# A recurrence in three operations per step with one source in PSUM, its scratch bank opened behind the parameters, and urgent rotary work for queries

## The chip, the cores and the metric

The kernel runs on one core of a Trainium2 chip. The metric is the device time of one execution in microseconds. Engines: PE is TensorE (matmul), DVE is VectorE, ACT is ScalarE, POOL is GpSimd, SP is SyncE, whose queue issues most DMAs.

## What is computed

One backbone layer over 1024 latent tokens and 256 context tokens of width 1024, in float32. A projection of the modulated, normed input gives queries, keys, values, the input of a state space model (S5) and gates:

```python
z = modulate(x, p['norm1_w'], sh1, sc1) @ w_in
q = rms_norm(z[..., Q_OFF:K_OFF].reshape(b, l, N_HEADS, 2, HEAD_DIM), p['q_norm_w'])
k = rms_norm(z[..., K_OFF:V_OFF].reshape(b, l, N_HEADS, 2, HEAD_DIM), p['k_norm_w'])
v = z[..., V_OFF:U_OFF].reshape(b, l, N_HEADS, V_DIM)
u = z[..., U_OFF:G_OFF]
g = z[..., G_OFF:]
q = rope_2d(q, rope)
k = rope_2d(k, rope)
...
y_attn = diff_head_out(blocked_latent_diff_attention(q, k_all, v_all, lam),
                       p['subln_w'], lam_init, p['w_branch_attn'])
y_s5, y_s5_c = s5_branch(u, uc, p, update_ctx)
x = x + ga1 * merge_branches(g, y_s5, y_attn, p['b_gate'], p['w_out'])
x = x + ga2 * conv_ffn(modulate(x, p['norm2_w'], sh2, sc2), p['w_up'], p['conv_w'], p['conv_b'], p['w_down'])
```

The S5 branch is a complex diagonal recurrence s' = a s + b u per channel group, once forwards and once backwards over the tokens, that starts from the final state of the context.

## The kernel before, in words

Every projection is made with operands split into a high and a low part: three matmuls (`whi,hTh`, `wlo,hTh`, `whi,hTl`; L418 to L420) for each of 8 slices of the width, so 24 of 512 columns for one tile `z` of 128 tokens by 512 outputs (`project`). `load_slab` loads a weight slab of 512 outputs as four pieces `wraw`; ScalarE makes `whi` of it, GpSimd `wlo` (L597).

`phase_a` takes the slabs in this order: U; K (two slabs, 10 tiles each: 8 of latent, 2 of context tokens); V (two, 10 tiles each); Q (two, 8 tiles each); then the gates G (four slabs, L555 to L557). `phase_b` is the attention and `phase_c` the feed-forward part; neither is touched.

While K runs, the generator `params` (`s5_params`) makes the matrices of the S5 branch. VectorE computes `ba` and `ca` (L753 to L758, last L841); TensorE transposes `ba` (L846) and multiplies `ca` and `sc` into a bank named `ada` (L864). The S5 branch works on chunks of 8 tokens: `s5_states_in` brings the input of every chunk into `X` (while V runs), and `s5_scan` then carries the state over 158 chunks, each step in four operations of VectorE on [128, 64] (L936 to L939), the factors `A8a` and `A8b` in SBUF. `phase_a` asks for ten steps per V tile once the states are there, for six steps per Q tile, and for the rest after Q.

For each Q tile, `qk_post` does the norm and the rotary part: ScalarE squares `z`; VectorE sums (L642), makes the mean square (L643), and after ScalarE's root the reciprocal and a correction (L647 to L650); VectorE multiplies `z` by the cosine and the sine table (L654, L658); GpSimd adds the two (L659) and scales by `qr` (L665); TensorE transposes the result `t` into `ta` or `tb` (L669); ScalarE and VectorE write it as a high and a low part `st` (L672, L673), which go to DRAM as `Qd`.

Between Q tiles stand pieces of `ada_part`, the modulation of the later stages: each loads 512 KB (`araw`, two buffers) and multiplies it into the bank `ada` (L297). Gate tiles are evicted by ScalarE into `stage` (L559).

PSUM has 8 banks: two of the pool `psT` (`ta`, `tb`), and in `psA` five buffers `z` and one `ada` in this part.

The order of the instructions on each engine is not written by hand here. A scheduler sets it when the program is built, from the program order, priorities and its own notion of when operands come; the hardware then runs each engine's instructions strictly in that order. A tile is the unit of its dependencies: two users of one tile keep their program order. A pool that is closed hands its memory on, and what is opened in its place waits for the last use of what was there.

Of the kernel before, what the change touches and what calls it, by code (L numbers as in the profile page):

```python
# [13 lines left out]
OP = mybir.AluOpType  # L14
AX = mybir.AxisListType
PSUM = bass.MemoryType.PSUM
DRAM = bass.MemoryType.DRAM

P = 128
# [8 lines left out]
HD = 64  # L28
G = 32
# [5 lines left out]
EPS = 1e-6  # L35
# [103 lines left out]
class Kern:  # L139
# [81 lines left out]
    def consts(self):  # L221
        nc, cp = self.nc, self.cp
        self.small = self.t(cp, [P, NSM], "small")
        self.ident = self.t(cp, [P, P], "ident")
        self.ones = self.t(cp, [P, P], "ones")
        nc.vector.memset(self.ones, 1.0)
        self.onesr = self.t(cp, [P, P], "onesr", 1, F32R)
        nc.vector.tensor_copy(self.onesr, self.ones)
        self.modT = self.t(cp, [P, 48, 2], "modT")
        self.neglam = self.t(cp, [P, 1], "neglam")  # L230
        self.hbg = self.t(cp, [P, 16], "hbg")
        self.hglub = self.t(cp, [P, 4], "hglub")
        self.subw = self.t(cp, [P, 1], "subw")
        self.scan_at = 0
# [78 lines left out]
    def phase_a(self):  # L313
        nc, cp, I = self.nc, self.cp, self.I
        self.psT, self.psT_st = self.pool("psT", space=PSUM)
        ps, ps_st = self.pool("psA", space=PSUM)
        ca, ca_st = self.pool("ca")
        self.mask = self.t(ca, [P, GC], "mask")
        self.rows = self.t(ca, [P, 384], "rows")
        self.s5c = self.t(ca, [P, 3, G], "s5c")  # L320
        self.A8a = self.t(ca, [P, 2, G], "A8a")
        self.A8b = self.t(ca, [P, 2, G], "A8b")
        hp, hp_st = self.pool("hT")
        hc, hc_st = self.pool("hTc", "right")
        hTh = [self.t(hp, [P, L], f"hTh{k}", 1, F32R) for k in range(KT)]
# [83 lines left out]
                nc.vector.scalar_tensor_tensor(l, x, self.modT[:, k, r:r + 1], r32(h), op0=OP.add, op1=OP.subtract)  # L409

        def project(tt, W, pz=None, ks=range(KT)):
            pz = self.t(ps, [P, 512], "z", 5) if pz is None else pz
            A = (hTh, hTl) if tt < NT else (cTh, cTl)
            tok = slice(tt % NT * P, tt % NT * P + P)
            for k in ks:
                wh, wl = W[0][k // 2][:, k % 2], W[1][k // 2][:, k % 2]
                hh, hl = A[0][k][:, tok], A[1][k][:, tok]
                nc.tensor.matmul(pz, hh, wh, start=k == 0, stop=False)  # L418
                nc.tensor.matmul(pz, hh, wl, start=False, stop=False)  # L419
                nc.tensor.matmul(pz, hl, wh, start=False, stop=k == KT - 1)  # L420
            return pz

        W = ([], [])
# [14 lines left out]
        def part_u(qt, tt):  # L438
            first[tt] = project(tt, W, first[tt], (2 * qt, 2 * qt + 1))
# [53 lines left out]
        def stage(pz):  # L493
            x = self.t(gp, [P, 512], "stage", 2)
            nc.scalar.copy(x, pz)
            return x
# [9 lines left out]
        zp, zp_st = self.pool("pk")  # L506
        self.rope_tables(zp, "K")
        for s in (0, 1):
            W = self.load_slab(wp, s)
# [4 lines left out]
        zp_st.close()  # L514
        for _ in params:
            pass
        xp, xp_st = self.pool("s5x")
        states = self.s5_states_in(xp, ps)
        next(states)
        for s in (2, 3):  # L520
            W = self.load_slab(wp, s)
            for tt in range(NKT):
                v = stage(project(tt, W))
# [7 lines left out]
        zp, zp_st = self.pool("pq")  # L531
        self.rope_tables(zp, "Q")
        adas = (st for grp in (1, 2) for st in self.ada_part(ap_, ps, crep, grp))
        for s in (5, 6):
            W = self.load_slab(wp, s)
            for tt in range(NT):
                self.qk_post(zp, ps, project(tt, W), "Q", s - 5, tt)
                next(adas, None)
                self.s5_scan(xp, self.scan_at + 6)
        zp_st.close()  # L540
# [4 lines left out]
        for s in range(7, 11):  # L545
            W = self.load_slab(wp, s)
            for mm in range(4):
                m = (s - 7) * 4 + mm
                for hf in range(2):
                    tok = slice(hf * 512, hf * 512 + 512)  # L550
                    pz = self.t(ps, [P, 512], "z", 5)
                    for k in range(KT):
                        wh = W[0][k // 2][:, k % 2, mm * P:mm * P + P]
                        wl = W[1][k // 2][:, k % 2, mm * P:mm * P + P]
                        nc.tensor.matmul(pz, wh, hTh[k][:, tok], start=k == 0, stop=False)  # L555
                        nc.tensor.matmul(pz, wh, hTl[k][:, tok], start=False, stop=False)
                        nc.tensor.matmul(pz, wl, hTh[k][:, tok], start=False, stop=k == KT - 1)  # L557
                    g = self.t(gp, [P, 512], "stage", 2)
                    nc.scalar.activation(g, pz, AF.Tanh, scale=0.5, bias=self.hbg[:, m:m + 1])  # L559
                    nc.scalar.dma_start(self.Gd[m][:, tok], g)  # L560
                    next(adas, None)
                    if hf and nq < QUADS:
                        if nq % 2 == 0:
                            Yq = self.t(yp, [P, NT, P], "Yq", 1)
                        with self.tc.high_priority():
                            self.s5_out_quad(yp, ps, nq, Yq, xp)
                            nq += 1
                            if nq % 2 == 0:
                                self.s5_transpose(yp, ps, Yq, nq // 2 - 1)
                        if nq == QUADS:  # L570
                            for _ in adas:
                                pass
                            ap_st.close()
                            yp_st.close()
                            xp_st.close()
                            tail = self.s5_tail(ps)
                    elif tail:
                        next(tail, None)
# [56 lines left out]
    def qk_post(self, zp, ps, pz, kind, hs, tt):  # L635

        nc = self.nc
        zv = pz.rearrange("p (h d) -> p h d", h=8)
        sq = self.t(zp, [P, 8, HD], "sq", 1)
        nc.scalar.activation(sq, zv, AF.Square)  # L640
        v = self.t(zp, [P, 8], "qv", 2)
        nc.vector.tensor_reduce(v, sq, axis=AX.X, op=OP.add)  # L642
        nc.vector.tensor_scalar(v, v, 1.0 / HD, EPS, op0=OP.mult, op1=OP.add)  # L643
        r = self.t(zp, [P, 8], "qr", 2)
        tm = self.t(zp, [P, 8], "qt", 2)
        nc.scalar.activation(tm, v, AF.Sqrt)
        nc.vector.reciprocal(r, tm)  # L647
        nc.vector.tensor_tensor(tm, r, r, op=OP.mult)
        nc.vector.scalar_tensor_tensor(tm, tm, -0.5, v, op0=OP.mult, op1=OP.mult)
        nc.vector.scalar_tensor_tensor(r, tm, 1.5, r, op0=OP.add, op1=OP.mult)  # L650
        t1 = self.t(zp, [P, 8, HD], "t1", 2)
        if tt < NT:
            ct, st = self.tabs[kind]
            nc.vector.tensor_tensor(t1, zv, ct[:, None, tt].to_broadcast([P, 8, HD]), op=OP.mult)  # L654
            t2 = self.t(zp, [P, 8, 2, 32], "t2", 2)
# [104 lines left out]
    def s5_params(self, ps):  # L760
        nc, I = self.nc, self.I
        sp, sp_st = self.pool("s5p", "right")
        self.lam(sp)
        V = nc.vector
# [10 lines left out]
        s, c = self.sincos_dve(sp, xi, n)  # L775
        pw = self.t(sp, [P, 2, 9, n], "pw")
# [26 lines left out]
            V.tensor_tensor(f[:, i], f[:, i], den, op=OP.mult)  # L803

        for i in range(2):
            V.tensor_copy(self.A8a[:, i], pw[:, 0, 8])
        V.tensor_scalar(self.A8b[:, 0], pw[:, 1, 8], -1.0, None, op0=OP.mult)
        V.tensor_copy(self.A8b[:, 1], pw[:, 1, 8])

        pin = self.t(sp, [P, 2, 8, n], "pin")  # L810
        pout = self.t(sp, [P, 2, 8, n], "pout")
# [5 lines left out]
        for q in range(QUADS):  # L817
            yield
            E = nc.vector if q % 2 or q == 6 else nc.gpsimd
# [11 lines left out]
            ca = self.t(sp, [P, 2, 4, 8, GC], "ca", 1)  # L831
# [28 lines left out]
            for o, w, x in ((0, blk[:, 0], ca), (P + GC, blk[:, 1], ca), (P, dup, sc)):  # L860
                for i in range(2):
                    for g in range(4):
# [8 lines left out]
                                   op0=OP.mult, op1=OP.add)  # L871
# [3 lines left out]
    def s5_states_in(self, xp, ps):  # L875

        nc = self.nc
        pp, pp_st = self.pool("s5in", "right")
        self.X = self.t(xp, [P, NCH + NCC, 2, G], "X")
        X = self.X  # L880
        NCK = NCH + NCC
        us, uts, wis = {}, {}, {}
        for step in range(QUADS + 2):
# [30 lines left out]
            if q >= 0:  # L914
                for g in range(4):
                    gg = 4 * q + g
                    px = self.pst([P, 2, NCK]) if g % 2 else self.t(ps, [P, 2, NCK], "z", 5)
                    for i in range(2):
                        nc.tensor.matmul(px[:, i], wis[q][:, i, g], uts[q][:, g], start=True, stop=True)
                    xo = X[:, :, :, gg].rearrange("p n i -> p i n")  # L920
                    nc.scalar.copy(xo[0:64, :, 0:NCC], px[0:64, :, NCH:])
                    nc.scalar.copy(xo[0:64, :, NCC:], px[0:64, :, 0:NCH])
                    nc.vector.tensor_copy(xo[64:128], px[64:128, :, ::-1])
# [3 lines left out]
    def s5_scan(self, xp, upto):  # L927

        nc, X = self.nc, self.X
        E = nc.vector.tensor_tensor  # L930
        upto = min(upto, NCH + NCC - 1)
        while self.scan_at < upto:
            i = self.scan_at
            t1 = self.t(xp, [P, 2, G], "sc1", 2)
            t2 = self.t(xp, [P, 2, G], "sc2", 2)
            E(t1, X[:, i - 1], self.A8a, op=OP.mult)  # L936
            E(t2, X[:, i - 1, ::-1], self.A8b, op=OP.mult)
            E(X[:, i], X[:, i], t1, op=OP.add)
            E(X[:, i], X[:, i], t2, op=OP.add)  # L939
            self.scan_at += 1  # L940

    def s5_out_quad(self, sp, ps, q, Yq, xp):
# [766 lines left out]
```

## Time and profile before

| what | us |
|---|---|
| time, median of 3 runs | 2119.36 (2116.5 to 2119.44) |
| the profiled execution | 2117.7, of it the span 2115.9 |
| TensorE busy | 2016.6 (95%) |
| VectorE busy | 1364.6 (64%) |
| ScalarE busy | 840.7 (40%) |
| GpSimd busy | 915.0 (43%) |

The span runs from the first to the last instruction of the profiled execution; all starts below are counted from its beginning. Busy time is a sum over stages with different limits. In the timeline "x4" behind a row counts instructions drawn together, and a bracket gives the idle time before the row and who ended it.

### The profile page before, as it was taken

What the parts mean: (1) busy time and instruction counts of PE and PEld (TensorE: products, weight loads), DVE (VectorE), ACT (ScalarE), POOL (GpSimd) and SP (SyncE); (2) the same over time, 40 slices, a digit from 0 to 9 for tenths busy, and PEclk for the clock granted to TensorE, in tenths of its full rate; (3) what the DMA queues carried; (4) which work ended last, traced back from release to release, by engine and by line L of the source; (5) the groups of instructions that cost most, each with busy time, mean ns of one, the idle gap of its engine ahead of it and who ended that gap; (6) DMA issues with size and microseconds to landing.
All of it is one profiled execution on the core that took longest, in us unless ns stands there. A gap on an engine that the chain in (4) does not pass through costs nothing.

```text
span 2115.9 us, 29038 instructions
## 1 busy us (share of the span) xinstructions
PE 2016.6 (95%) x10392; PEld 1643.8 (78%) x10392; DVE 1364.6 (64%) x2591; ACT 840.7 (40%) x1509; POOL 915.0 (43%) x1009
## 2 busy tenths in 40 slices
PE   6988999998999999999999989987999999999999
PEld 4766778866678887999999878765888888878887
DVE  6988944799972133888888654468777777752222
ACT  4434424221222312788888611343444443432100
POOL 1466411233311531366666745643544444455321
PEclk9998999999999999999999999987999999999999
DMA  9345575345667326322331135432222222254212
GB/s 325 111 112 140 123 204 182 111 133 163 186 198 232 112 100 225 112 83 78 94 107 53 39 131 177 151 90 70 100 80 79 82 82 79 80 193 129 67 55 93
DMA packets 164624, 262.48 MB, mean 124 GB/s; under 512 B 28672, under 2 KB 92544, under 8 KB 164480
## 3 DMA queue, kind: packets, MB, share of 16 engines
q1 hardware_dynamic: 154400, 242.28, 37.0%
q10 hardware_dynamic: 10080, 18.35, 2.3%
q8 instruction: 82, 1.34, 0.3%
q14 instruction: 62, 0.51, 0.1%
HBM read 188.68 MB, written 71.89 MB: 123 GB/s over the span
## 4 chain that ended last, share of the span: by engine, by line
PE 70%; DVE 21%; DMA 4%; issue 3%; POOL 1%; ACT 1%; SPq 0%; DVEq 0%; ACTq 0%; POOLq 0%
PE ta L1040 7%; PE d L1268 4%; PE d L1269 4%; PE d L1267 4%; PE up L1488 4%; PE up L1489 4%; PE up L1487 4%; PE sc L1240 3%; PE sc L1241 3%; PE z L1487 3%; PE z L1489 3%; PE z L1488 3%; PE tb L1022 3%; DVE X L939 2%; DVE sc L936 2%
## 5 line engine op out<-in xcount | busy, mean ns | idle before, releaser
L1242 DVE TENSOR_REDUCE mx<-sc 128x1 f32<-128x1280 f32 x128 | 190.7, 1491 | 53.3 <-PE sc L1241 52.3
L597 POOL TENSOR_TENSOR wlo<-wraw,whi 128x1024 fp32r<-128x1024 f32 x40 | 97.3, 2449 | 245.8 <-ACT whi L596 243.8
L418 PE MATMUL z<-whi,hTh 128*128 128x512 f32 x448 | 183.1, 413 | 3.6 <-ACT hTh L407 3.6
L419 PE MATMUL z<-wlo,hTh 128*128 128x512 f32 x448 | 181.7, 407 | 0.3 <-POOL wlo L597 0.3
L420 PE MATMUL z<-whi,hTl 128*128 128x512 f32 x448 | 179.9, 403 | 0.0
L995 ACT ACTIVATE e<-sc,mx 128x1280 f32<-128x1280 f32 x128 | 171.9, 1343 | 12.3 <-DVE mx L1242 10.6
L1664 DVE SCALAR_TENSOR_TENSOR x1b<-d,modT,x1b 128x512 f32<-128x512 f32 x80 | 59.8, 750 | 181.3 <-PE d L1269 181.3
L1040 PE MATMUL ta<-V,at 128*128 128x128 f32 x1280 | 168.1, 275 | 0.7 <-ACT at L1029 0.7
L1040 PEld LDWEIGHTS ta<-V,at 128*128 128x128 f32 x1280 | 155.4, 191 | 1.0 <-ACT at L1029 0.9
L1240 PE MATMUL sc<-K,q 128*128 128x512 f32 (+1 forms) x384 | 147.7, 385 | 0.8 <-ACT e L995 0.8
L1480 POOL TENSOR_TENSOR pl<-s,ph 128x512 fp32r<-128x512 f32 x44 | 65.0, 1479 | 182.5 <-ACT ph L1479 182.5
L1268 PE MATMUL d<-g,whi 128*128 128x512 f32 x352 | 139.8, 397 | 3.1 <-DVE g L1636 3.1
L1685 DVE SCALAR_TENSOR_TENSOR y<-up,small,y 128x896 f32<-128x896 f32 (+1 forms) x176 | 123.7, 744 | 29.5 <-ACT y L1680 28.1
L1267 PE MATMUL d<-g,whi 128*128 128x512 f32 x352 | 139.5, 396 | 0.0
L1269 PE MATMUL d<-g,wlo 128*128 128x512 f32 x352 | 139.3, 396 | 0.0
L1241 PE MATMUL sc<-K,q 128*128 128x512 f32 (+1 forms) x384 | 131.9, 358 | 0.0
L1255 POOL TENSOR_TENSOR wlo<-wraw,whi 128x1024 fp32r<-128x1024 f32 (+1 forms) x36 | 74.9, 2087 | 122.5 <-ACT whi L1254 111.6
L418 PEld LDWEIGHTS z<-whi,hTh 128*128 128x128 f32 x448 | 87.1, 194 | 33.1 <-issue 9.8
L1660 POOL TENSOR_TENSOR wlo<-wraw,whi 128x640 fp32r<-128x640 f32 (+2 forms) x40 | 56.3, 1407 | 116.3 <-ACT whi L1659 115.3
L555 PE MATMUL z<-hTh,whi 128*128 128x512 f32 x256 | 102.4, 400 | 0.0
L420 PEld LDWEIGHTS z<-whi,hTl 128*128 128x128 f32 x448 | 87.3, 195 | 19.3 <-issue 1.0
L419 PEld LDWEIGHTS z<-wlo,hTh 128*128 128x128 f32 x448 | 87.5, 195 | 17.4 <-POOL wlo L597 0.7
(490 smaller groups left out, 5509.0 us busy)
## 6 DMA issues: line engine op xcount, KB each, us to landing
wraw<-in_wup_dram SPq DMA_DIRECT2D x46, 512.0 KB
wraw<-in_win_dram SPq DMA_DIRECT2D x44, 512.0 KB
araw<-in_ada_dram SPq DMA_DIRECT2D x32, 512.0 KB
q<-Qd SPq DMA_DIRECT2D x128, 128.0 KB
Kd<-st SPq DMA_DIRECT2D x80, 128.0 KB
K<-Kd SPq DMA_DIRECT2D x16, 640.0 KB
Fd<-y SPq DMA_DIRECT2D x20, 512.0 KB
graw<-Fd SPq DMA_DIRECT2D x20, 512.0 KB
```

The source lines that it names most:

```text
L418: nc.tensor.matmul(pz, hh, wh, start=k == 0, stop=False)
L419: nc.tensor.matmul(pz, hh, wl, start=False, stop=False)
L420: nc.tensor.matmul(pz, hl, wh, start=False, stop=k == KT - 1)
L995: nc.scalar.activation(em, S[i]["sc"][m][:, :LK], AF.Exp, bias=S[i]["mx"][:, m:m + 1], accum_out=S[i]["l1"] if m else S[i]["l0"])
L1040: nc.tensor.matmul(PO[p][:, j * P:j * P + P], AT[p, kt // 2][:, kt % 2, j * P:j * P + P], W[:, kt], start=kt == 0, stop=kt == NKT - 1)
L1240: nc.tensor.matmul(sc[:, a:b], Q[0][:, m, qs], K[m][:, a:b], start=True, stop=False)
L1241: nc.tensor.matmul(sc[:, a:b], Q[1][:, m, qs], K[m][:, a:b], start=False, stop=True)
L1242: nc.vector.tensor_reduce(S["mx"][:, m:m + 1], sc[:, :LK], axis=AX.X, op=OP.max, negate=True)
L1267: mm(o, W[0][:, k], ah[k], start=k == 0, stop=False)
L1268: mm(o, W[0][:, k], al[k], start=False, stop=False)
L1269: mm(o, W[1][:, k], ah[k], start=False, stop=k == n - 1)
L1487: mm(o, W[0][:, k], bh[k], start=k == 0, stop=False)
```

## The change

1. A scan step takes three operations. The first multiplies the state, read twice, by both factor pairs (`A8`, now one tile of [128, 2, 2, 32], copied into PSUM as `A8p`) into a piece of PSUM; the second and third add the two halves to `X`, the second half with its pair exchanged.
2. After the parameters are done the PSUM pool is closed and a new one, `psA2`, is opened with four buffers `z` instead of five and one bank `scr`. In `scr` lie `A8p`, two products of the scan, and the statistics of Q tiles.
3. `qk_post` runs under high priority for Q; its sum and reciprocal lie in `scr` (four sets in rotation), and the correction squares nothing any more but reads the reciprocal from PSUM. For K the same code uses one more small tile, `qi`.

```diff
+        ps_st.close()
+        ps, ps_st = self.pool("psA2", space=PSUM)
+        nz = 4
+        scr = self.t(ps, [P, 512], "scr", 1)
+        self.A8p = scr[:, 0:128].rearrange("p (j i g) -> p j i g", j=2, i=2)
+        self.scT = [scr[:, 128 * j:128 * j + 128].rearrange("p (j i g) -> p j i g", j=2, i=2) for j in (1, 2)]
+        self.qkp = [[scr[:, 384 + 32 * b + 8 * j:392 + 32 * b + 8 * j] for j in range(2)] for b in range(4)]
+        self.qkn = 0
+        nc.vector.tensor_copy(self.A8p, self.A8)
         xp, xp_st = self.pool("s5x")
         states = self.s5_states_in(xp, ps)
...
-                self.qk_post(zp, ps, project(tt, W), "Q", s - 5, tt)
+                pz = project(tt, W)
+                with self.tc.high_priority():
+                    self.qk_post(zp, ps, pz, "Q", s - 5, tt)
                 next(adas, None)
                 self.s5_scan(xp, self.scan_at + 6)
...
-        nc.vector.tensor_reduce(v, sq, axis=AX.X, op=OP.add)
-        nc.vector.tensor_scalar(v, v, 1.0 / HD, EPS, op0=OP.mult, op1=OP.add)
+        vp, rp = self.qkp[self.qkn % 4] if kind == "Q" else (v, self.t(zp, [P, 8], "qi", 2))
+        self.qkn += 1
+        nc.vector.tensor_reduce(vp, sq, axis=AX.X, op=OP.add)
+        nc.vector.tensor_scalar(v, vp, 1.0 / HD, EPS, op0=OP.mult, op1=OP.add)
...
-        nc.vector.reciprocal(r, tm)
-        nc.vector.tensor_tensor(tm, r, r, op=OP.mult)
-        nc.vector.scalar_tensor_tensor(tm, tm, -0.5, v, op0=OP.mult, op1=OP.mult)
-        nc.vector.scalar_tensor_tensor(r, tm, 1.5, r, op0=OP.add, op1=OP.mult)
+        nc.vector.reciprocal(rp, tm)
+        nc.vector.scalar_tensor_tensor(tm, rp, -0.5, v, op0=OP.mult, op1=OP.mult)
+        nc.vector.tensor_tensor(tm, rp, tm, op=OP.mult)
+        nc.vector.scalar_tensor_tensor(r, tm, 1.5, rp, op0=OP.add, op1=OP.mult)
...
-            t1 = self.t(xp, [P, 2, G], "sc1", 2)
-            t2 = self.t(xp, [P, 2, G], "sc2", 2)
-            E(t1, X[:, i - 1], self.A8a, op=OP.mult)
-            E(t2, X[:, i - 1, ::-1], self.A8b, op=OP.mult)
-            E(X[:, i], X[:, i], t1, op=OP.add)
-            E(X[:, i], X[:, i], t2, op=OP.add)
+            t = self.scT[i % 2]
+            E(t, X[:, i - 1, None].to_broadcast([P, 2, 2, G]), self.A8p, op=OP.mult)
+            E(X[:, i], X[:, i], t[:, 0], op=OP.add)
+            E(X[:, i], X[:, i], t[:, 1, ::-1], op=OP.add)
```

The change moves instructions on every engine. Three places follow, as the built programs order them (line number, operation, destination <- sources, shape, count; the numbers behind names tell buffers apart). First TensorE where V begins, in the program before: `ca_482` and `sc_477` belong to the last matrix of the parameters, and `z_570` is the fifth V tile.

```order
L420 MATMUL z_570_3126<-whi_551_2992,hTl1_24_113 128x512
L418 MATMUL z_570_3126<-whi_554_2998,hTh2_17_106 128x512
L864 MATMUL ada_489_2586<-ca_482_2548,blk_487_2579 32x128 x16
L864 MATMUL ada_489_2586<-sc_477_2535,dup_488_2581 32x16 x8
L419 MATMUL z_570_3126<-wlo_555_2999,hTh2_17_106 128x512
L420 MATMUL z_570_3126<-whi_554_2998,hTl2_25_114 128x512
```

The same place in the changed program: `ca_495` and `sc_490` are that last matrix, `z_582` is the first V tile, and `tb_555` and `ta_565` are transposes of the last K tiles.

```order
L860 MATMUL ada_407_2107<-ident_2_74,ba_403_2083 128x128 x4
L878 MATMUL ada_411_2122<-ca_404_2084,blk_409_2115 32x128 x16
L878 MATMUL ada_411_2122<-sc_399_2071,dup_410_2117 32x16 x8
L683 MATMUL tb_555_2928<-ident_2_74,t1_554_2919 128x128 x4
L860 MATMUL ada_496_2576<-ident_2_74,ba_494_2560 128x128 x4
L683 MATMUL ta_565_2988<-ident_2_74,t1_564_2979 128x128 x4
L860 MATMUL ada_498_2584<-ident_2_74,ba_494_2560 128x128 x4
L878 MATMUL ada_502_2599<-ca_495_2561,blk_500_2592 32x128 x16
L878 MATMUL ada_502_2599<-sc_490_2548,dup_501_2594 32x16 x8
L419 MATMUL z_582_3039<-whi_571_3017,hTh0_14_103 128x512
```

Before, 103 matmuls of the first five V tiles stand ahead of the last pair; now none does. Second, VectorE at the first Q tile, in the program before, where 41 steps of the scan stand ahead of the first reduction and steps and tile work alternate.

```order
L937 TENSOR_TENSOR sc2_789_4174<-X_549_2989,A8b_14_97 128x64
L642 TENSOR_REDUCE qv_868_4474<-sq_867_4472 128x8
L654 TENSOR_TENSOR t1_871_4484<-z_866_4447,CQ_852_4417 128x512
L938 TENSOR_TENSOR X_549_2989<-X_549_2989,sc1_788_4173 128x64
L658 TENSOR_TENSOR t2_872_4486<-z_866_4447,SQ_853_4418 128x512
L643 TENSOR_SCALAR qv_868_4474<-qv_868_4474 128x8
L939 TENSOR_TENSOR X_549_2989<-X_549_2989,sc2_789_4174 128x64
```

The same in the changed program: 70 steps stand ahead of the first reduction, six follow each tile's work (the last three rows are the first of them), and the two products L668 and L672 of a tile stand in the work of the tile before.

```order
L951 TENSOR_TENSOR X_569_3014<-X_569_3014,scr_568_3006 128x64
L656 TENSOR_REDUCE scr_568_3006<-sq_747_4287 128x8
L657 TENSOR_SCALAR qv_748_4289<-scr_568_3006 128x8
L668 TENSOR_TENSOR t1_763_4376<-z_758_4339,CQ_732_4232 128x512
L672 TENSOR_TENSOR t2_764_4378<-z_758_4339,SQ_733_4233 128x512
L661 RECIPROCAL scr_568_3006<-qt_750_4293 128x8
L662 SCALAR_TENSOR_TENSOR qt_750_4293<-scr_568_3006,qv_748_4289 128x8
L663 TENSOR_TENSOR qt_750_4293<-scr_568_3006,qt_750_4293 128x8
L664 SCALAR_TENSOR_TENSOR qr_749_4292<-qt_750_4293,scr_568_3006 128x8
L949 TENSOR_TENSOR scr_568_3006<-X_569_3014,scr_568_3006 128x128
L950 TENSOR_TENSOR X_569_3014<-X_569_3014,scr_568_3006 128x64
L951 TENSOR_TENSOR X_569_3014<-X_569_3014,scr_568_3006 128x64
```

The tile work of Q and the scan no longer overlap. Third, TensorE between the fifth and the sixth Q tile, before (`z_959` and `z_982`).

```order
L420 MATMUL z_959_4824<-whi_864_4443,hTl7_30_119 128x512
L297 MATMUL ada_876_4501<-araw_969_4878,crep_47_142 32x512 x2
L418 MATMUL z_982_4918<-whi_855_4425,hTh0_15_104 128x512
L419 MATMUL z_982_4918<-wlo_856_4426,hTh0_15_104 128x512
L420 MATMUL z_982_4918<-whi_855_4425,hTl0_23_112 128x512
L669 MATMUL tb_920_4679<-ident_2_74,t1_918_4673 128x128 x4
```

And in the changed program (`z_791` and `z_802`), where nine pieces of the modulation stand together.

```order
L421 MATMUL z_791_4567<-whi_744_4258,hTl7_29_118 128x512
L298 MATMUL ada_756_4316<-araw_801_4621,crep_46_141 32x512 x2
L298 MATMUL ada_756_4316<-araw_812_4697,crep_46_141 32x512 x2
L298 MATMUL ada_756_4316<-araw_823_4773,crep_46_141 32x512 x2
L298 MATMUL ada_756_4316<-araw_834_4849,crep_46_141 32x512 x2
L298 MATMUL ada_756_4316<-araw_857_4949,crep_46_141 32x512 x2
L298 MATMUL ada_756_4316<-araw_868_5025,crep_46_141 32x512 x2
L298 MATMUL ada_756_4316<-araw_879_5101,crep_46_141 32x512 x2
L298 MATMUL ada_756_4316<-araw_890_5177,crep_46_141 32x512 x2
L298 MATMUL ada_756_4316<-araw_901_5253,crep_46_141 32x512 x2
L419 MATMUL z_802_4643<-whi_735_4240,hTh0_14_103 128x512
```

In the changed program four such pieces stand ahead of these nine, two behind the sixth tile and one behind the seventh; the transposes of the first Q tile stand in the sixth tile behind 21 of its matmuls, those of each later tile five tiles behind it, so that the last five of sixteen come among the gate tiles.

## Rows read from the trace of the kernel before

**Rows 1.** Windows: us, busy us (instructions) of PE, PEld, DVE, ACT, POOL; clock; DMA.

```profile
300.00:325.00 25.00, 25.00 (x133) 20.90 (x131) 6.42 (x12) 7.91 (x21) 0.00 (x0) 1.00 0.67 190
550.00:575.00 25.00, 20.08 (x78) 12.81 (x77) 23.57 (x109) 5.78 (x9) 4.68 (x3) 0.86 0.80 238
575.00:600.00 25.00, 25.00 (x108) 16.83 (x107) 23.22 (x107) 5.92 (x7) 4.52 (x2) 1.00 0.57 182
```

**Rows 2.** Waits of PE, 383 to 620: us in total, times, longest.

```profile
PE ta L669 <- POOL t L665: 5.6, 3, 4.2
...
PE ada L297 <- DMA araw<-in_ada_dram: 4.0, 2, 3.2
```

**Rows 3.** Timeline of DVE, first Q tile and a later one: start us, us.

```profile
426.99 0.68 DVE L642 TENSOR_REDUCE qv<-sq 128x8 f32<-128x512 f32 x1
...
481.77 0.68 DVE L642 TENSOR_REDUCE qv<-sq 128x8 f32<-128x512 f32 x1
482.37 0.68 DVE L654 TENSOR_TENSOR t<-z,CQ 128x512 f32<-128x512 f32 x1
```

**Rows 4.** Timeline of DVE, the first scan step.

```profile
383.50 0.23 DVE L936 TENSOR_TENSOR sc<-X,A8a 128x64 f32<-128x64 f32 x1
383.65 0.22 DVE L937 TENSOR_TENSOR sc<-X,A8b 128x64 f32<-128x64 f32 x1
...
384.04 0.23 DVE L939 TENSOR_TENSOR X<-X,sc 128x64 f32<-128x64 f32 x1
384.29 0.23 DVE L936 TENSOR_TENSOR sc<-X,A8a 128x64 f32<-128x64 f32 x1
```

**Rows 5.** Timelines of POOL and DVE, 407 to 411.

```profile
407.75 7.14 POOL L597 TENSOR_TENSOR wlo<-wraw,whi 128x1024 fp32r<-128x1024 f32 x3 [57.45 <-ACT whi L596]
...
407.94 2.33 DVE L936 TENSOR_TENSOR sc<-X,A8a 128x64 f32<-128x64 f32 x1
```

**Rows 6.** Groups of DVE, 383 to 620 (busy us, mean ns); source L939 (min/median/max).

```profile
L939 DVE TENSOR_TENSOR X<-X,sc 128x64 f32<-128x64 f32 x158 | 53.8, 341 | 4.2
...
L654 DVE TENSOR_TENSOR t<-z,CQ 128x512 f32<-128x512 f32 x16 | 10.8, 675 | 0.0
...
L939 DVE TENSOR_TENSOR X<-X,sc x158: 209/224/2432, 384.0 to 608.6; 128x64 f32<-128x64 f32 x158
```

**Rows 7.** Timeline of DVE, two operations of the parameters.

```profile
95.05 0.28 DVE L755 TENSOR_TENSOR pw<-pw,ptmp 128x128 f32<-128x128 f32 x1
...
298.50 0.23 DVE L870 SCALAR_TENSOR_TENSOR kq<-mask,small,ada 128x16 f32<-128x16 f32 x1 [10.79 <-ACT kq L868]
```

**Rows 8.** Timeline of PE, start of V and the last parameter pair.

```profile
261.56 0.39 PE L418 MATMUL z<-whi,hTh 128*128 128x512 f32 x1
...
296.79 1.08 PE L864 MATMUL ada<-ca,blk 128*32 128x128 f32 x32
...
297.92 0.50 PE L419 MATMUL z<-wlo,hTh 128*128 128x512 f32 x1
```

**Rows 9.** Timeline of DVE, the last operations on `ca`.

```profile
286.55 0.69 DVE L758 TENSOR_TENSOR ca<-ca,tq 128x512 f32<-128x512 f32 x1
287.28 0.43 DVE L841 TENSOR_SCALAR ca<-ca 128x512 f32<-128x512 f32 x1
```

**Rows 10.** Timeline of PE, first Q tile and first gate tile.

```profile
410.50 0.39 PE L418 MATMUL z<-whi,hTh 128*128 128x512 f32 x1
...
411.18 0.39 PE L418 MATMUL z<-whi,hTh 128*128 128x512 f32 x1
...
537.75 0.50 PE L555 MATMUL z<-hTh,whi 128*128 128x512 f32 x1
```

**Rows 11.** Timelines of SP and PE, a modulation piece that came late.

```profile
481.29 1.12 SPq L294 DMA_DIRECT2D araw<-in_ada_dram  x2
...
486.26 1.05 PE L297 MATMUL ada<-araw,crep 128*32 128x512 f32 x4 [3.19 <-DMA araw<-in_ada_dram]
487.24 0.66 PE L418 MATMUL z<-whi,hTh 128*128 128x512 f32 x1
```

More of the change, by code (lines that the diff above doesn't have):

```diff
@@ L316, in phase_a @@
         ps, ps_st = self.pool("psA", space=PSUM)
+        nz = 5
         ca, ca_st = self.pool("ca")
@@ L320, in phase_a @@
         self.s5c = self.t(ca, [P, 3, G], "s5c")
-        self.A8a = self.t(ca, [P, 2, G], "A8a")
-        self.A8b = self.t(ca, [P, 2, G], "A8b")
+        self.A8 = self.t(ca, [P, 2, 2, G], "A8")
         hp, hp_st = self.pool("hT")
@@ L411, in project @@
         def project(tt, W, pz=None, ks=range(KT)):
-            pz = self.t(ps, [P, 512], "z", 5) if pz is None else pz
+            pz = self.t(ps, [P, 512], "z", nz) if pz is None else pz
             A = (hTh, hTl) if tt < NT else (cTh, cTl)
@@ L516, in phase_a @@
             pass
+        ps_st.close()
[5 more added lines that the diff above has]
+        self.qkp = [[scr[:, 384 + 32 * b + 8 * j:392 + 32 * b + 8 * j] for j in range(2)] for b in range(4)]
+        self.qkn = 0
+        nc.vector.tensor_copy(self.A8p, self.A8)
         xp, xp_st = self.pool("s5x")
@@ L550, in phase_a @@
                     tok = slice(hf * 512, hf * 512 + 512)
-                    pz = self.t(ps, [P, 512], "z", 5)
+                    pz = self.t(ps, [P, 512], "z", nz)
                     for k in range(KT):
@@ L805, in s5_params @@
         for i in range(2):
-            V.tensor_copy(self.A8a[:, i], pw[:, 0, 8])
-        V.tensor_scalar(self.A8b[:, 0], pw[:, 1, 8], -1.0, None, op0=OP.mult)
-        V.tensor_copy(self.A8b[:, 1], pw[:, 1, 8])
+            V.tensor_copy(self.A8[:, 0, i], pw[:, 0, 8])
+        V.tensor_copy(self.A8[:, 1, 0], pw[:, 1, 8])
+        V.tensor_scalar(self.A8[:, 1, 1], pw[:, 1, 8], -1.0, None, op0=OP.mult)
         pin = self.t(sp, [P, 2, 8, n], "pin")
@@ L916, in s5_states_in @@
                     gg = 4 * q + g
-                    px = self.pst([P, 2, NCK]) if g % 2 else self.t(ps, [P, 2, NCK], "z", 5)
+                    px = self.pst([P, 2, NCK]) if g % 2 else self.t(ps, [P, 2, NCK], "z", 4)
                     for i in range(2):
```

## The prediction

> **What bounds the kernel now.** I read the windows first, then the waits of TensorE, then the timelines of TensorE and VectorE at the two places where the change moves work. The windows [rows 1] show TensorE without a gap where the V slabs run (300 to 325) and in the later gate slabs (575 to 600), but only 20.08 us busy of 25 at a granted clock of 0.86 where queries hand over to gates (550 to 575); VectorE is busy 23.57 there. The waits [rows 2] say for whom TensorE stops between 383 and 620: for `t` of the rotary work (5.6 us of the `ta` wait) and for `araw` of the modulation (4.0). Behind `t` stands VectorE, which between the first query tile's reduction at 426.99 and the start of the gate slabs at 537.75 [rows 3] does both the queries' work and the scan. So up to the end of V the kernel is bound by TensorE, in Q by VectorE, with TensorE close behind, and from the gates on by TensorE again. A shift of the first gate tile is a shift of the end, unless a wait behind it is swallowed.
>
> **Part 1, the scan step.** Undisturbed, four operations take 0.79 us: one step starts at 383.50, the next at 384.29, and an operation that needs the one before it starts some 0.25 us after it (384.04 to 384.29 [rows 4]). Disturbed they take far longer: while GpSimd makes `wlo` from 407.75 on, one of them takes 2.33 [rows 5]. Over the 158 steps L939 has a mean of 341 ns, against a median of 224; L654, which reads PSUM, has 675 at 512 elements [rows 6] and shows no such stretch (an unstretched SBUF operation of that size, L758, takes 0.69 [rows 9]). The new step is a 128-element product into PSUM and two dependent 64-element additions, each with one source in PSUM. The trace has no such product; a 128-element one in SBUF takes 0.28 [rows 7], 0.06 over 64 elements, so its successor should start 0.31 to 0.32 after it. I take 0.32 + 0.255 + 0.255 = 0.83 us. Undisturbed that is no gain; what goes is the stretch. Below, I bound it by 0.70, if the additions follow each other at the 0.15 of independent ones (383.50 to 383.65 [rows 4]) in part; above, by 0.98: L870, 16 elements with one source in PSUM, takes 0.23 [rows 7], as long as 64 elements in SBUF, so that 0.05 more for each of three operations is possible. I stay at 0.83, as the 512-element rows put PSUM and SBUF on a level.
>
> The stretch falls on operations with two sources in SBUF and spares those that read PSUM [rows 5, 6]. [...]
>
> **Part 2, the bank opened behind the parameters.** The old PSUM pool is closed before the first V tile, so its last reader comes first. The order shows it: on TensorE 103 V matmuls now stand behind the last `ca`/`sc` pair that stood ahead of it. Before, the first of them ran at 261.56, filling the time in which VectorE made the parameters, and the pair at 296.79, followed by V at 297.92 [rows 8]. The pair's own operand is ready much sooner: VectorE ends `ca` at 287.28 + 0.43 = 287.71 [rows 9]. Now TensorE idles up to there, does the pair at the lower clock (1.6 for its 1.13 [rows 8]), and starts V at 289.3. The 103 matmuls take 103 x 0.227 = 23.4 us (0.227 from 410.50 to 411.18 for three [rows 10]), and 2.0 more because after the idle time the clock is granted late (after the 3.19 us wait at 486.26 a matmul took 0.66 instead of 0.39 [rows 11]). That is 314.7, where before it was 297.9: **16.8 us late**. TensorE has no gap from 300 to 325, so nothing takes this back: the scan's start goes from 383.50 to 400.3 and Q's first matmul from 410.50 to 427.3. Bounds: 14.5 (no cold clock) and 18.5 (cold for nearly twice as long).
>
> **Part 3, the queries' work.** That is urgent now, but its statistics share one tile with the scan, so VectorE runs the two strictly in program order: 70 steps before the first reduction (41 before), then six for each tile. The first reduction comes at 400.3 + 70 x 0.83 + 1.2 for two rotary products = 459.6, instead of 426.99 [rows 3].
>
> TensorE meanwhile: five query tiles of 24 x 0.227 = 5.44 and four pieces of modulation (`ada`) at 0.98 (486.26 to 487.24 [rows 11]) end at 427.3 + 31.1 = 458.4. Then the order shows nine pieces in a row ahead of the sixth tile, where before one stood between each two tiles. Each needs 512 KB in one of two buffers; from the issue at 481.29 to TensorE's release at 486.26 it took 4.97 us [rows 11], under load. Two landed ahead; seven more come two per round of 4.5 + 1, so the burst takes some **20 us** (12 to 23, by a round of 3.4 to 6): the sixth tile starts at 478.4. Without the burst it would wait for VectorE's product of the second tile, to 461.9. The transposes of the first tile stand behind 21 of its matmuls, cold at first: 478.4 + 4.8 + 1.7 = 484.9. VectorE waits for them at `st`, then does six steps and the rest of a tile's work (8.3, below); with 1.3 allowed for ScalarE's copy and the handovers the third reduction comes at 494.5.
>
> From there VectorE sets the pace: four operations of 512 elements at 0.60 (481.77 to 482.37 [rows 3]) and 0.9 for the small ones, 3.3, and six steps, 5.0, are 8.2 to 8.3 us per tile; TensorE needs only 5.44 + 0.98 and a few tenths for transposes. The twelfth reduction is at 494.5 + 9 x 8.2 = 568.3, and the first gate tile, which takes the bank that the thirteenth query tile frees 1.9 later, at 570.3 instead of 537.75 [rows 10]: **+32.6 us**.
>
> Behind that: three more transposes stand among the gate tiles (+1.1); the second gate tile takes the bank of the first and waits for its eviction, behind late roots on ScalarE, with table loads (+3.8; 0.9 to 6); a wait of 4.2 before, the longest of [rows 2], with 2.0 of cold matmuls goes, since VectorE is then ahead (-6.2). The scan ends at about 606, where its last operation started at 608.6 [rows 6], so it adds nothing. The root and its correction keep their number of operations, K's extra tile costs nothing, and the copy of A8 into PSUM, 128 elements, lies in VectorE's free time up to 298.50, where its next operation waits [rows 7]. **Sum: 32.6 + 1.1 + 3.8 - 6.2 = +31.3 us.** The profiled execution took 2117.7, so I get 2149; the median of the runs shown, 2119.36, is 1.7 above that execution.
>
> **The rivals.**
> *The burst hardly binds and the step is cheap* (20%). If the nine pieces take 12 us and the step 0.70, the sixth tile starts at 470.4, the third reduction comes 15 later, a tile takes 7.5, and the first gate tile starts at 485.4 + 9 x 7.5 + 1.9 = 554.8: +17.1 - 1.3 gives 2133. With the lower bounds of part 2 (-2.3) and of the second gate tile (-2.9) this case reaches from 2128 to 2140. For it: an idle queue may land a transfer faster than the loaded one I read.
> *VectorE no longer binds in Q* (8%), the faster side. Mechanism: the scan is freed of GpSimd's stretches, and TensorE alone paces Q. Four transposes of 128 columns should take a quarter of four modulation matmuls of 512, 0.25; so 16 x (5.44 + 0.98) + 11 x 0.25 = 105.5 us from 427.3 is 532.8, 5.0 ahead of 537.75, and with the old wait and cold matmuls gone (-6.2) about 2107. It decides if VectorE's work per tile, six steps included, comes under 6.7 us and the burst does not hold the transposes back. Against it: 8.2 per tile, and the order.
> *PSUM operands are dearer* (12%). At 0.98 per step and 0.05 more for six small operations, a tile takes 9.5: third reduction at 495.5, first gate tile at 495.5 + 85.5 + 1.9 = 582.9, +45.2 - 1.3, so 2162. [...]
> *The change does not do what it says* (3%): GpSimd goes on stretching the steps, as one source still lies in SBUF. Then 0.12 for each operation, by which the mean of L939 exceeds its median [rows 6], comes on top: 3 x 6 x 0.12 = 2.1 us per tile, 19 over nine, about 2168.
> *Nothing moves in sum* (7%): the late V start, against a Q phase shorter by as much, 2114 to 2122.
>
> **How the numbers follow.** My own case has 50%, with 2140 to 2157 by its bounds. The range holds it, the cheap case with 2 us to spare, and the dear one: 2126 to 2163. What a measurement of this kernel can tell from no change is about 0.2%, 4 us. Faster by more than that: the second rival and a little of the last, 0.10; within it: the rest of the last, 0.06; slower: 0.84.
>
> **What would show it.** TensorE all but idle from 262 to 289 and the scan's first step near 400; no L949 to L951 over 0.4 us; nine modulation pieces in a row around 458 to 478, each pair behind a DMA; VectorE waiting for `ta` or `tb` near 475 to 485; the first gate tile near 570 and from there the old pace. I would be wrong if V started before 280, if the step measured under 0.7 or over 0.95, or if the burst passed in under 12 us.

## The result, and the profile after

| kernel | us, median | ratio to before, 95% interval |
|---|---|---|
| before | 2119.4 | |
| changed | 2172.57 (2169.99 to 2173.76) | 1.0248 [1.0229, 1.0267] |

The change makes the kernel 53 us slower. The direction was forecast, the size was not: 2149 was said, and the range ended at 2163. The profiled execution took 2172.82 us, its span 2171.0, so 55.1 more than the span before.

The windows of the changed kernel, with the columns of [rows 1], show where: TensorE has gaps at the start of V (250 to 300, granted clock 0.67 to 0.79) and through the whole of Q (450 to 600, at 0.80 to 0.93), and in Q VectorE is not full either.

```profile
250.00:275.00 25.00, 11.86 (x105) 8.65 (x104) 24.92 (x45) 11.46 (x28) 12.92 (x8) 0.79 0.57 154
...
300.00:325.00 25.00, 25.00 (x115) 20.62 (x114) 0.78 (x2) 3.60 (x7) 0.00 (x0) 1.00 0.14 50
...
475.00:500.00 25.00, 20.52 (x80) 11.77 (x76) 8.07 (x27) 1.81 (x4) 2.29 (x2) 0.80 0.49 149
...
550.00:575.00 25.00, 18.56 (x67) 14.58 (x68) 19.91 (x73) 2.58 (x6) 6.87 (x6) 0.80 0.16 43
```

The waits of TensorE from 400 to 680, against [rows 2] (383 to 620): it no longer waits for GpSimd's `t`, but for the rotary products of VectorE (L672) and for `araw`.

```profile
PE z L419 <- DVE t L672: 18.2, 7, 4.6
PE ada L298 <- DMA araw<-in_ada_dram: 11.6, 6, 4.0
PE z L567 <- DVE scr L661: 6.4, 1, 6.4
PE z L419 <- DVE scr L661: 5.6, 2, 3.2
PE z L567 <- ACT stage L571: 1.7, 1, 1.7
```

And VectorE waits for TensorE and ScalarE in the same stretch (waits of VectorE, 398 to 640, the three longest, in total, times, longest):

```profile
DVE t L668 <- PE tb L683: 14.9, 1, 14.9
DVE st L687 <- ACT st L686: 14.1, 10, 2.2
DVE t L668 <- ACT sq L652: 6.7, 3, 5.7
```

The scan step itself came out as forecast. The sources L949 to L951 (min/median/max in ns, first and last start) show nothing over 298 ns, where L939 had 2432 [rows 6]; the next step starts 0.84 us after the first (398.83 to 399.67).

```profile
L949 DVE TENSOR_TENSOR scr<-X,scr x158: 295/295/298, 398.8 to 628.1; 128x128 f32<-128x128 f32 x158
...
L951 DVE TENSOR_TENSOR X<-X,scr x158: 211/220/223, 399.4 to 628.6; 128x64 f32<-128x64 f32 x158
```

Three starts on TensorE's timeline answer to [rows 8], [rows 11] and [rows 10]: V's first matmul, the end of the nine modulation pieces, and the first gate tile.

```profile
287.72 0.41 PE L878 MATMUL ada<-sc,dup 128*32 128x16 f32 x16
288.06 0.80 PE L419 MATMUL z<-whi,hTh 128*128 128x512 f32 x1
...
457.98 1.07 PE L298 MATMUL ada<-araw,crep 128*32 128x512 f32 x8
463.07 3.16 PE L298 MATMUL ada<-araw,crep 128*32 128x512 f32 x8 [4.03 <-DMA araw<-in_ada_dram]
...
482.15 0.80 PE L419 MATMUL z<-whi,hTh 128*128 128x512 f32 x1
...
592.52 0.76 PE L567 MATMUL z<-hTh,whi 128*128 128x512 f32 x1 [6.40 <-DVE scr L661]
```

The scan starts 15.3 us late (398.83 against 383.50 [rows 4]) and the gates 54.8 (592.52 against 537.75 [rows 10]). So 39.5 us arise between them, and hardly anything (0.3) behind.

Where those come from is seen in the reductions of VectorE, one for each tile, and in one tile's time. First VectorE (the third, fourth and twelfth reduction, then the stretch around 530), then TensorE around 530:

```profile
498.58 0.68 DVE L656 TENSOR_REDUCE scr<-sq 128x8 f32<-128x512 f32 x1
507.13 0.69 DVE L656 TENSOR_REDUCE scr<-sq 128x8 f32<-128x512 f32 x1
...
587.63 0.70 DVE L656 TENSOR_REDUCE scr<-sq 128x8 f32<-128x512 f32 x1
```

```profile
526.21 0.69 DVE L656 TENSOR_REDUCE scr<-sq 128x8 f32<-128x512 f32 x1
526.94 0.17 DVE L657 TENSOR_SCALAR qv<-scr 128x8 f32<-128x8 f32 x1
528.64 0.69 DVE L687 TENSOR_TENSOR st<-tb,st 128x512 fp32r<-128x512 f32 x1 [1.53 <-ACT st L686]
...
529.84 0.68 DVE L672 TENSOR_TENSOR t<-z,SQ 128x512 f32<-128x512 f32 x1
...
536.31 0.69 DVE L656 TENSOR_REDUCE scr<-sq 128x8 f32<-128x512 f32 x1
...
538.23 0.69 DVE L668 TENSOR_TENSOR t<-z,CQ 128x512 f32<-128x512 f32 x1 [1.02 <-PE ta L683]
```

```profile
527.34 0.60 PE L683 MATMUL tb<-ident,t 128*128 128x128 f32 x4
...
530.58 0.79 PE L419 MATMUL z<-whi,hTh 128*128 128x512 f32 x1 [2.41 <-DVE t L672]
...
537.49 0.60 PE L683 MATMUL ta<-ident,t 128*128 128x128 f32 x4
```

The product that ends at 530.5 frees a z bank; TensorE starts its tile at 530.58, at a granted clock of 0.50 up to 533 (the first matmul takes 0.79 us instead of 0.39); the transposes of an older tile stand behind 23 of its 24 matmuls, at 537.49; and VectorE's next product (538.23), whose `t` buffer they free, waits for them. Neither engine is full, each waits for the other in turn: a ring. From the third reduction (498.58) to the last (628.89) a tile takes 10.0 us.

### The profile page after: what moved, and what is told of

Read it like the earlier page. It is cut to its first block, busy times and chain, and to the rows that moved or that the text cites. A ratio compares the mean times of both kernels' runs of the same rounds, so it can differ in the third digit from the quotient of the medians.

```text
span 2171.0 us, 28883 instructions
## 1 busy us (share of the span) xinstructions
PE 2026.9 (93%) x10392; PEld 1651.4 (76%) x10392; DVE 1328.7 (61%) x2434; ACT 849.3 (39%) x1515; POOL 911.4 (42%) x1009
## 4 chain that ended last, share of the span: by engine, by line
PE 64%; DVE 4%; issue 3%; DMA 3%; POOL 1%; ACT 1%; SPq 0%; DVEq 0%; POOLq 0%; ACTq 0%
PE ta L1052 7%; PE up L1500 3%; PE up L1499 3%; PE up L1501 3%; PE sc L1252 3%; PE sc L1253 3%; PE d L1281 3%; PE d L1279 3%; PE d L1280 3%; PE z L567 3%; PE z L569 3%; PE z L568 3%; PE tb L1034 3%; PE z L1499 3%; PE z L1501 3%
## 5 line engine op out<-in xcount | busy, mean ns | idle before, releaser
L1007 ACT ACTIVATE e<-sc,mx 128x1280 f32<-128x1280 f32 x128 | 172.0, 1344 | 12.3 <-DVE mx L1254 10.5
L673 POOL TENSOR_TENSOR t<-t,t 128x512 f32<-128x512 f32 x32 | 43.4, 1356 | 162.1 <-DVE t L672 80.1
```

The costliest lines, as they stand in the source:

```text
L1007: nc.scalar.activation(em, S[i]["sc"][m][:, :LK], AF.Exp, bias=S[i]["mx"][:, m:m + 1], accum_out=S[i]["l1"] if m else S[i]["l0"])
```

## The experiments

The theory after the result: (a) the closed pool makes V late; (b) one scratch tile for the scan and the queries' statistics forces their program order on VectorE, and out of that come both the burst of nine pieces and the ring; (c) the step itself gains. The rivals: four z banks starve TensorE; operands in PSUM are dear; the late V is swallowed. The high priority mark is no candidate: without it the changed kernel is ordered row for row alike on all five engines.

**ada in a pool of its own.** The bank that `s5_params` and `ada_part` use comes from a pool `pb`, so that the pool closed before V holds only z banks.

```diff
+        pb, pb_st = self.pool("psB", space=PSUM)
         ps, ps_st = self.pool("psA", space=PSUM)
...
-        params = self.s5_params(ps)
+        params = self.s5_params(pb)
```

> The changed kernel, with the bank of the modulation and the parameters (ada) in a PSUM pool of its own, so that the pool that is closed before V holds z banks alone. Theory (late V, then a lockstep): V starts near 262 again, the scan 13 to 16 us earlier than in the changed kernel (398.8), the query phase keeps its burst and its pace of 10 us per tile, and all of the 13 to 16 us arrives at the end: 2157 to 2160. Rival (the late V is swallowed, because the query phase waits for something else): scan earlier, but 2170 to 2173.

Measured: 2162.04, ratio 1.0192 [1.0173, 1.0212], 10.5 us under the changed kernel and 2 above the range expected. The scan starts at 392.44, 6.4 us earlier, not 13 to 16: V begins at 275.57, since its first tile gets a bank of a late K tile (3.62 us of waiting for `t` in the row below). So (a) holds for the start of V, and the expectation missed the second half of its lateness. What the lateness costs at the end this run does not show: of the 6.4 us only 2.9 stand at the first gate tile (589.62 against 592.52), and the rest of the 10.5 arises behind it, for a reason that stays open. The run after the next shows the cost without the ring.

```profile
271.30 0.65 PE L880 MATMUL ada<-ca,blk 128*32 128x128 f32 x8 [6.58 <-ACT wi L864]
...
275.57 0.80 PE L420 MATMUL z<-whi,hTh 128*128 128x512 f32 x1 [3.62 <-DVE t L677]
...
589.62 0.47 PE L568 MATMUL z<-hTh,whi 128*128 128x512 f32 x1 [1.34 <-DVE scr L663]
```

**The statistics in SBUF.**

```diff
-        vp, rp = self.qkp[self.qkn % 4] if kind == "Q" else (v, self.t(zp, [P, 8], "qi", 2))
+        vp, rp = v, self.t(zp, [P, 8], "qi", 2)
```

> The changed kernel, with the sums and reciprocals of the queries in SBUF as before, so that the scratch tile in PSUM belongs to the scan alone. V stays late. Theory (one shared tile forces program order, and with it the burst and the lockstep): 38 steps ahead of the first reduction instead of 70, no nine modulation pieces in a row, the first gate tile at 531 to 548 instead of 592.5, time 2113 to 2130. Rival (four z banks instead of five starve TensorE): the first gate tile after 570, time above 2150.

Measured: 2113.33, ratio 0.9965 [0.9954, 0.9977]: one line turns 53 us of loss into 7 of gain, with V as late as in the changed kernel (287.63). The gates start at 537.7, the nine pieces no longer stand together, and TensorE's waits from 400 to 680 shrink to these:

```profile
537.71 0.50 PE L567 MATMUL z<-hTh,whi 128*128 128x512 f32 x1
...
PE tb L976 <- ACT yst L1209: 1.9, 1, 1.9
PE ada L298 <- DMA araw<-in_ada_dram: 0.3, 1, 0.3
```

There are four z banks here too, so that rival falls.

**Both.** The two edits above together.

> Both: ada in its own pool, and the queries' statistics in SBUF. What is left of the change is the three-operation step and one z bank less. Theory: the two gains add, 13 to 16 us below the run with statistics in SBUF alone, 2098 to 2115, under the kernel before (2119). Rival (four z banks): no better than 2135. Rival (the step in PSUM gains nothing of itself): 2117 to 2122.

Measured: 2105.87, ratio 0.9926 [0.9906, 0.9947]. Faster than before, with 7.5 us from the separate pool (not 13 to 16, for the same wait for a K bank). The scan starts 8.7 us earlier than in the run with the statistics in SBUF alone (389.15 against 397.83), and the first gate tile too (529.03 against 537.71), so nothing of the late V is swallowed here. From 400 to 680 TensorE's list of waits is empty.

**The old step, everything else as changed.**

```diff
-            t = self.scT[i % 2]
-            E(t, X[:, i - 1, None].to_broadcast([P, 2, 2, G]), self.A8p, op=OP.mult)
-            E(X[:, i], X[:, i], t[:, 0], op=OP.add)
-            E(X[:, i], X[:, i], t[:, 1, ::-1], op=OP.add)
+            t1 = self.t(xp, [P, 2, G], "sc1", 2)
+            t2 = self.t(xp, [P, 2, G], "sc2", 2)
+            E(t1, X[:, i - 1], self.A8[:, 0], op=OP.mult)
+            E(t2, X[:, i - 1, ::-1], self.A8[:, 1, ::-1], op=OP.mult)
+            E(X[:, i], X[:, i], t1, op=OP.add)
+            E(X[:, i], X[:, i], t2, op=OP.add)
```

> The changed kernel with the old step of four operations in SBUF; the bank is still opened behind the parameters and the queries' statistics still lie in PSUM, but the scan no longer shares a tile with them. Theory: only the late V is left, 15 us, and a query phase as before: first gate tile near 553, time 2130 to 2138. Rival (four z banks, or the statistics in PSUM, make the loss in Q): above 2150.

Measured: 2135.32, ratio 1.0068 [1.0044, 1.0092]; the gates start at 552.0. The statistics in PSUM alone do no harm, the scan in PSUM alone does none (the run with statistics in SBUF): only both in one tile do. A kernel with both in PSUM but in two tiles was not run; that it is the common tile, and not PSUM with two users, rests on the order of the instructions and on the scan's operations, which take as long in the run with the statistics in SBUF as in the changed kernel (medians of 296, 221 and 221 ns against 295, 220 and 220).

**Four buffers for t1.** `"t1"` with 4 buffers instead of 2 for Q.

> The changed kernel with four buffers instead of two for the rotary product t1 of the queries; order nearly unchanged. In the changed kernel VectorE's product waits for the transposes that free its buffer (14.9 + 4.1 us) and its st for ScalarE's copy of the transposes (14.1), while TensorE waits for the product. Theory (a ring: product, 21 matmuls, transposes, next product): one link opens, the st link stays, the pace falls from 10.0 to between 8.5 and 9.5 us per tile, 2158 to 2168. Rival (the pace is VectorE's own work and the cold clock, no ring): 2171 to 2174.

Measured: 2163.45, ratio 1.0199 [1.0184, 1.0215]. VectorE's wait for `ta` and `tb` is gone from the product. The long wait behind the burst (14.9 before) now stands at `st`, as 14.4 of the first row below; the other nine waits of `st` for ScalarE's copy of the transposes are 11.7 us, against 14.1 in ten:

```profile
DVE st L687 <- ACT st L686: 26.1, 10, 14.4
DVE t L668 <- ACT sq L652: 12.2, 12, 6.0
```

The pace is (621.41 - 497.44) / 13 = 9.5 us, against 10.0. One link opened, and the other stayed, as expected.

**No modulation between queries.** The pool of `araw` is opened behind Q, so no piece can come earlier.

```diff
-                next(adas, None)
                 self.s5_scan(xp, self.scan_at + 6)
...
+        ap_, ap_st = self.pool("pada")
+        adas = (st for grp in (1, 2) for st in self.ada_part(ap_, ps, crep, grp))
         yp, yp_st = self.pool("s5y")
```

> The changed kernel with all pieces of the modulation issued behind Q (their memory is opened there), so that none stands between query tiles; they crowd into the gate slabs instead, which costs more there, so only the query phase is read. Theory (the burst holds the first transposes back by 15 us, the lockstep by 2 us per tile is a cause of its own): third reduction at 480 to 487 instead of 498.6, pace still 9.5 to 10.5, first gate tile at 572 to 582 instead of 592.5. Rival (the burst fills a time in which TensorE would wait anyway): first gate tile at 588 to 593.

Measured once: third reduction at 481.90, first gate tile at 572.9 (2201.52 in all, as the pieces crowd into the gates, where TensorE waits 18.1 for `araw`).

```profile
481.90 0.69 DVE L655 TENSOR_REDUCE scr<-sq 128x8 f32<-128x512 f32 x1
...
572.93 0.47 PE L566 MATMUL z<-hTh,whi 128*128 128x512 f32 x1 [1.34 <-DVE scr L660]
```

That is 16.7 and 19.6 us earlier than in the changed kernel; but the scan starts 2.7 earlier too (396.11), so the burst costs some 14 to 17 us. The ring goes on without it, at (607.25 - 481.90) / 13 = 9.6 per tile.

**The step's own worth.** The kernel with both mends, but the old step in SBUF:

> As the run with ada in its own pool and the statistics in SBUF, but with the old step of four operations in SBUF: what is left of the change is one z bank less and the reopened pool. Theory: V 6 us late as in that run, the query phase as in the kernel before: 2119 to 2128, so that the step is worth 13 to 22 us of the 2105.9. Rival (the gain of that run is from another order, not from the step): 2104 to 2110.

Measured: 2128.35, ratio 1.0038 [1.0025, 1.005], just above the range expected. Against 2105.87 the step is worth 22 us; what is left of the change (the reopened pool and the missing bank above all) costs 8 against the kernel before.

**Three operations, in SBUF.** Product and factors in SBUF, five z banks, no pool reopened.

```diff
-            t = self.scT[i % 2]
+            t = self.t(xp, [P, 2, 2, G], "sc", 2)
```

> The step in three operations, but product and factors in SBUF; five z banks, no pool reopened, statistics in SBUF. Theory (the gain of the step is that its operations no longer have two sources in SBUF): its operations are stretched while GpSimd runs, maxima above 2 us, and the time is 2112 to 2120, a few us under the kernel before at best. Rival (the gain is from three operations instead of four): 2096 to 2106, without the 6 us by which V is late.

Measured: 2123.38, ratio 1.0013 [1.0001, 1.0026], a little above the range expected. The sources of its operations:

```profile
L941 DVE TENSOR_TENSOR sc<-X,A x158: 276/292/2389, 387.7 to 615.4; 128x128 f32<-128x128 f32 x158
...
L943 DVE TENSOR_TENSOR X<-X,sc x158: 208/225/2382, 388.3 to 615.9; 128x64 f32<-128x64 f32 x158
```

The medians are close to those of the step in PSUM, the maxima to those of before. From the scan's first operation to the first gate tile 151.2 us pass here (387.68 to 538.87), 152.8 with the old step in the run above (390.68 to 543.43) and 139.9 with the step in PSUM in the run with both mends (389.15 to 529.03). So fewer operations alone gain next to nothing; the source in PSUM does. Why the scan starts 4.2 us later here than before (383.50), with no pool reopened, stays open.

**Reopening at the fifth V tile.** Both mends, and the pool is closed and reopened where the K tiles' banks are long free.

```diff
+                if s == 2 and tt == 4:
+                    ps_st.close()
+                    ps, ps_st = self.pool("psA2", space=PSUM)
+                    nz = 4
+                    self.psv = ps
+                    scr = self.t(ps, [P, 512], "scr", 1)
...
                 v = stage(project(tt, W))
```

> As the run with ada in its own pool and the statistics in SBUF, but the z pool is closed and reopened with four banks and the scratch bank before the fifth V tile instead of the first, when the products of the last K tiles have long freed the old banks. Theory (what is left of the late V is TensorE's wait for a z bank of K behind the busy VectorE): the scan starts at 383 to 385 instead of 389.4, TensorE has no gap in Q, and 4 to 6 us arrive at the end: 2099 to 2102. Rival (a later wait swallows them): 2104 to 2107.

Measured: 2099.4, ratio 0.9896 [0.9879, 0.9912], the best version: 21 us under the kernel before. The scan starts at 383.3, as before, and the first gate tile at 523.2, 14.6 us earlier. TensorE has no wait between 400 and 680; its windows there are full at full clock:

```profile
500.00:525.00 25.00, 25.00 (x114) 16.96 (x114) 21.61 (x72) 8.32 (x14) 11.72 (x9) 1.00 0.54 156
525.00:550.00 25.00, 25.00 (x115) 18.00 (x113) 22.74 (x80) 6.95 (x10) 7.63 (x5) 1.00 0.76 237
```

## Why the prediction was right and wrong

*Part 1, the step:* right. 0.84 us measured for 0.83 forecast, no stretch left. The two rivals on it fall: PSUM operands are not dearer (the product has a median of 295 ns in PSUM and 292 in SBUF), and GpSimd stretches none: while it makes `wlo` from 504.33 to 511.39, the three steps from 504.61 to 507.10 take 0.22 to 0.30 us per operation. The last addition took 2382 ns at most with both sources in SBUF (L943 of the run with three operations in SBUF), and 223 with one of them in PSUM (L951).

*Part 2, the late V:* right in place and size. V at 288.06 for 289.3, the scan at 398.83 for 400.3.

*Part 3, up to the third reduction:* nearly right. The first reduction came at 464.42 for 459.6, since VectorE reached the first product 5.7 us before its tile was squared; the burst lasted 24.2 us for 20, just outside its bound of 23; the third reduction came at 498.58 for 494.5. So the rival in which the burst hardly binds falls. None of the three signs that the prediction gave for being wrong came (V at 288.06, the step at 0.84, the burst at 24.2); the pace behind the burst was not among them.

*The step that failed* is the sentence "From there VectorE sets the pace", with 8.2 us per tile and 568.3 for the twelfth reduction. Measured were (587.63 - 498.58) / 9 = 9.9, and 587.63. VectorE's own part was nearly as summed: from the third reduction to the fourth, where it waits for no transposes, a tile takes 8.55, of it 0.59 a wait for ScalarE's root. But the order that was known beforehand (transposes five tiles behind, at the end of a tile that waits for a product) puts TensorE's tile into VectorE's way. One turn of the ring, from 530.58 to 539.57, is TensorE's 6.9 for 23 matmuls, with a granted clock of 0.50 up to 533, then 0.7 us from the transposes to the product, and the product 1.3: 9.0. The turn before it, in which `st` waits for ScalarE's copy too, takes 10.1, and every second one after it 10.8, where `st`, the next reduction and ScalarE's root all stand ahead of the product. The prediction compared each engine's work per tile and took the larger; it did not follow the waits round. This makes 15 of the 22 us by which the first gate tile was missed; 4 are the late third reduction, and 3 the last step from the twelfth reduction to the gates (4.9 for 1.9).

*Behind the gates:* -1.3 was forecast, +0.3 measured. For the 3.8 us of the second gate tile's wait for its eviction the prediction shows no row; measured is 1.7 (the wait for `stage`); a table load on ScalarE took 1.28 (551.48 in the kernel before, 599.66 here). The old wait for `t` is gone, as forecast. How the rest adds up to +0.3 was not taken apart. Together 22.2 + 1.6 = 23.8 us, the difference of 2172.82 and 2149.

*The rivals:* the faster side's mechanism, VectorE freed of the stretches and TensorE alone in Q, was right as a mechanism. It was kept from acting by the shared tile; with that alone undone, and V still late, it is the run with the statistics in SBUF, 2113.33 for the 2107 worked out, its first gate tile at 537.7 for 532.8.

## What to carry to other kernels

Before putting small things into one scratch tile, ask what order its users then keep: two chains that share a tile run in program order, and what the scheduler had interleaved falls apart, here at 59 us (2172.57 against 2113.33). Where two engines hand each other tiles, follow one tile round from buffer to buffer before taking the larger of their loads as the pace. And where memory is reopened under a running engine, the place counts as much as the amount: reopening the bank of the parameters together with the z banks made the scan 15 us late, the z banks alone 6, and the z banks alone four tiles later not at all.

## What the runs showed of the hardware that was not expected

The step's operations took as long with one source in PSUM as with both in SBUF, at 64 and at 128 elements (medians of 220 against 225 ns, 295 against 292), and none of the 474 took over 298 ns, also while GpSimd made `wlo` (from 504.33 on, 7.06 us). In the ring TensorE lost part of its clock at short waits: after three of them in a row, of 2.4 to 2.7 us (up to 510.04, 520.48 and 530.58), the next matmul took 0.77 to 0.79 us and the following ones 0.63 instead of 0.39, at a granted clock of 0.50 (up to 512, 523 and 533); that of the windows fell to between 0.80 and 0.93. It does not go by the length of the wait alone: after 4.60 us (up to 550.37) the first two took 0.50 and 0.40, and only the next ones 0.59 and 0.63.
